# Two matmuls of 256 columns in place of one of 512, in the projections and the down products of a convolution and mixture-of-experts block

## The chip, the cores and the metric

The kernel runs on one core of one Trainium2 chip. The metric is the time of one execution on the device in microseconds (us); less is better. TensorE (PE in the profile) does the matmuls, and its weight loads have a row of their own (PEld). VectorE is DVE, ScalarE is ACT, GpSimd is POOL, and SyncE (SP) issues most of the DMAs.

## The reference, cut to what matters

There is one layer with 2048 tokens and 1024 channels, in float32: a gated short convolution between two projections, then a mixture of 16 experts, each of which takes the 256 tokens that score best for it.

```python
gate_b, gate_c, v = jnp.split(h @ w_in, 3, axis=-1)              # input projection, 1024 -> 3072
y = (gate_b * dwconv_centred(gate_c * v, conv_w)) @ w_out        # output projection, 1024 -> 1024
lat = lat + g1 * y
h2 = modulate(rms_norm(lat, norm_g[1]), sh2, sc2)
aff = jax.nn.softmax(h2 @ w_router)                              # 16 experts
g, idx = lax.top_k(jnp.swapaxes(aff, 1, 2), 256)
xs = h2[idx]                                                     # 256 rows for each expert
hid = jax.nn.silu(xs @ w_gate) * (xs @ w_up)                     # 1024 -> 1024, twice
ys = (hid @ w_down) * g                                          # 1024 -> 1024
lat = lat + g2 * scatter_add(ys, idx)
```

## The kernel before, in words

Every large product is made of three matmuls in the type fp32r: both operands are split into a rounded high part and the remainder, and high by high, high by low and low by high are added up in PSUM. `ws` tiles hold split weights, `hl` tiles the split activations of the mixer, `xT` and `hT` those of the experts. A matmul loads 128 columns of one operand into the array as weights (the stationary operand) and streams the columns of the other one past them (the moving operand). In the profile's `pm<-hl,ws` the first name is the moving operand and the second the stationary one.

- **Input projection** (`in_mm`, lines 436, 437, 439). For 32 combinations of a 128-channel block and a quarter of the tokens, eight steps k of nine products each: three weight matrices times three parts. Stationary: `ws`, 128x128. Moving: `hl`, 512 tokens. That is 2304 products. Each of the three outputs fills one PSUM bank of 512 float32 columns.
- **Output projection** (`out_mm`, lines 641, 642, 644). For 16 blocks of 128 tokens, eight steps of six products. Stationary: `hl`. Moving: `ws`, 512 columns. That is 768 products. Transposes (line 690) and the router's matmuls (lines 708 and 709, `hl` moving, 128 columns) stand between them.
- **Experts.** `gate_up` (lines 1010, 1012, 1014) has `ws` stationary and `xT`, 256 columns, moving: 6144 products. `down` (`product`, lines 1032 to 1034) has `hT` stationary and `ws`, 512 columns, moving: 1536 products in 32 calls. For each expert the order is half of `gate_up`, a `down` half of the expert before, the other half of `gate_up`, the other `down` half.

The order on every engine is that in which the code is written. The weights come by DMA into three buffers, are split by ACT (line 198) and DVE (line 208) into eight `ws` buffers, and are loaded some steps ahead of their use.

Of the kernel before, what the change touches and what calls it, by code (L numbers as in the profile page):

```python
# [21 lines left out]
KD = D // P  # L22
NB = L // P
NQ = 4
QT = L // NQ
# [15 lines left out]
def block_kernel(ctx: ExitStack, tc, x, c, ada_w, ada_b, norm_g, w_in, conv, w_out, router, wg, wu, wd, out):  # L41
    nc = tc.nc
# [57 lines left out]
    def constants(scratch):  # L100
        before = consts.tile([P, P], BF, name="before")
        nc.vector.tensor_scalar(before, jp, 0.0, None, op0=ALU.is_gt)
        ones_b = consts.tile([P, 1], BF, name="ones_b")
        nc.vector.memset(ones_b, 1.0)

        def group_of(name, shift, mask, pattern):

            row = consts.tile([P, 1], I32, name=name + "_i")
            nc.gpsimd.iota(row, pattern=[[0, 1]], base=0, channel_multiplier=1)
            nc.vector.tensor_scalar(row, row, shift, mask, op0=ALU.logical_shift_right, op1=ALU.bitwise_and)  # L110
            rowf = consts.tile([P, 1], F32, name=name + "_r")
            nc.vector.tensor_copy(rowf, row)
            n = 1
            for _, m in pattern:
                n *= m
            col = scratch("col", n)
            nc.gpsimd.iota(col, pattern=pattern, base=0, channel_multiplier=0, allow_small_or_imprecise_dtypes=True)
            t = consts.tile([P, n], F32R, name=name)
            nc.vector.tensor_scalar(t, col, rowf, None, op0=ALU.is_equal)
            return t, rowf  # L120

        same, _ = group_of("same", 3, E - 1, [[1, E], [0, 8]])
        sameq, _ = group_of("sameq", 3, NF - 1, [[0, P // (8 * NF)], [1, NF], [0, 8]])
        rep, repf = group_of("rep", 5, 3, [[1, 4]])
        block, _ = group_of("block", 5, 3, [[1, 4], [0, 32]])
        tri = consts.tile([P, P], BF, name="tri")
        nc.vector.tensor_mul(tri, block.bitcast(F32), before)
        mult = consts.tile([P, 5], F32, name="mult")
        nc.gpsimd.iota(mult, pattern=[[4, 5]], base=1, channel_multiplier=0, allow_small_or_imprecise_dtypes=True)
        nc.vector.tensor_scalar(mult, mult, repf, None, op0=ALU.add)  # L130
        stepq = consts.tile([P, N_FEW[0] + N_FEW[1], 3], F32, name="stepq")
        biasq = consts.tile([P, N_FEW[0] + N_FEW[1], 2], F32, name="biasq")
        for i in range(N_FEW[0] + N_FEW[1]):
            lo = i >= N_FEW[0]
            unit = 1.0 if lo else float(1 << LOW_FEW)
            st = unit * float(FEW) ** (N_FEW[0] + lo * N_FEW[1] - 1 - i)
            nc.gpsimd.tensor_scalar(stepq[:, i], mult[:, 0:3], st, None, op0=ALU.mult)
            nc.gpsimd.tensor_scalar(biasq[:, i], mult[:, 3:5], -st, 0.5 * unit, op0=ALU.mult, op1=ALU.add)
        needq = consts.tile([P, 5, 4], F32, name="needq")
        nc.gpsimd.memset(needq[:, 0:3], float(CAP))  # L140
        nc.gpsimd.memset(needq[:, 3:5], float(2 * CAP - L))
        slot_r = consts.tile([P, P], BF, name="slot_r")
        nc.gpsimd.iota(slot_r, pattern=[[1, P]], base=0, channel_multiplier=0,
                       allow_small_or_imprecise_dtypes=True)
        step = consts.tile([P, N_HI + N_LO], F32, name="step")
        bias = consts.tile([P, N_HI + N_LO, 2], F32, name="bias")
        for i in range(N_HI + N_LO):
            st = (1 << LOW) * 4.0 ** (N_HI - 1 - i) if i < N_HI else 4.0 ** (N_HI + N_LO - 1 - i)
            nc.gpsimd.memset(step[:, i:i + 1], st)
            for j in range(2):  # L150
                nc.gpsimd.memset(bias[:, i, j:j + 1], 0.5 * (float(1 << LOW) if i < N_HI else 1.0) - (j + 2) * st)
        need = consts.tile([P, 3], F32, name="need")
        nc.gpsimd.memset(need[:, 0:1], float(CAP))
        nc.gpsimd.memset(need[:, 1:3], float(2 * CAP - L))
        zero1 = consts.tile([P, 4], F32, name="zero1")
        nc.gpsimd.memset(zero1, 0.0)
        cnts = [consts.tile([P, 4], F32R, name=f"cnt{i}") for i in range(2)]
        for t in cnts:
            nc.vector.tensor_copy(t, zero1)
        zero1 = zero1[:, 0:1]  # L160
        aux = consts.tile([P, E, NB, 5], BF, name="aux")
        nc.gpsimd.iota(aux[:, :, :, 0], pattern=[[0, E], [0, NB]], base=0, channel_multiplier=1,
                       allow_small_or_imprecise_dtypes=True)
        nc.gpsimd.iota(aux[:, :, :, 1], pattern=[[0, E], [1, NB]], base=0, channel_multiplier=0,
                       allow_small_or_imprecise_dtypes=True)
        quick = sameq, rep, stepq, biasq, needq
        return before, ones_b, tri, slot_r, step, bias, need, zero1, cnts, aux, same, quick


    pieces, n_load, n_high, n_done = [], 0, 0, 0  # L170
# [177 lines left out]
    with tc.tile_pool(name="mix", bufs=1) as mix:  # L348
# [83 lines left out]
        def in_mm(ps, q, W, k):  # L432
            t = hl[q, k]
            for m in range(3):
                wh, wl = W(k, m)
                nc.tensor.matmul(ps[m], wh, t[:, 0], start=(k == 0), stop=False)  # L436
                nc.tensor.matmul(ps[m], wl, t[:, 0], start=False, stop=False)  # L437
            for m in range(3):
                nc.tensor.matmul(ps[m], W(k, m)[0], t[:, 1], start=False, stop=(k == KD - 1))  # L439

        def in_out(ps, q, ct):
            pb, pc, pv = ps
# [132 lines left out]
        for i, (ps_, ct, q) in enumerate(steps):  # L575
# [23 lines left out]
            ps = new_banks()  # L599
# [15 lines left out]
        def half(h):  # L615
            return slice(h * QT, (h + 1) * QT)
# [17 lines left out]
        def out_mm(tb, k, hs=(0, 1)):  # L634
            ps = ps_of.setdefault(tb, {})
            vh, vl = vs_of[tb]
            w = ws_of[w_o[k]]
            for h in hs:
                if k == 0:
                    ps[h] = mm.tile([P, QT], F32, name="pm", tag="mm")  # L640
                nc.tensor.matmul(ps[h], vh[:, k], w[:, 0, half(h)], start=(k == 0), stop=False)  # L641
                nc.tensor.matmul(ps[h], vh[:, k], w[:, 1, half(h)], start=False, stop=False)  # L642
            for h in hs:
                nc.tensor.matmul(ps[h], vl[:, k], w[:, 0, half(h)], start=False, stop=(k == KD - 1))  # L644

        def out_res(tb, h, soon=None):

# [378 lines left out]
    def down(e, dh, between=lambda kk: None):  # L1026
        ps = [mm.tile([P, H], F32, name="pm", tag="mm") for _ in range(2)]

        def product(s, k):
            w, j, t = ws_of[w_moe[2, e, dh, k // 2]], k % 2, slice(s * P, (s + 1) * P)  # L1030
            h, l = (hT_of[e][k // 4][:, i, k % 4, t] for i in range(2))
            nc.tensor.matmul(ps[s], h, w[:, 0, j], start=(k == 0), stop=False)  # L1032
            nc.tensor.matmul(ps[s], h, w[:, 1, j], start=False, stop=False)  # L1033
            nc.tensor.matmul(ps[s], l, w[:, 0, j], start=False, stop=(k == KD - 1))  # L1034

        for kk in range(KD // 2):
            between(kk)
            split_to(w_moe[2, e, dh, kk] + n_split - 1)
            if (e, dh) != (E - 1, 1):
                for k in (2 * kk, 2 * kk + 1):  # L1040
                    for s in range(2):
                        product(s, k)
        if (e, dh) == (E - 1, 1):
            for s in range(2):
                for k in range(KD):
                    product(s, k)
        if dh == 0:
            ot_of[e] = [moe.tile([P, D], F32, name="ot", tag="ot", bufs=3) for _ in range(2)]
        ots = ot_of[e]
        c0 = slice(dh * H, (dh + 1) * H)  # L1050
        for s in range(2):
            nc.vector.scalar_tensor_tensor(ots[s][:, c0], ps[s], gate_of[e][:, s:s + 1], g2b[:, c0],  # L1052
                                           op0=ALU.mult, op1=ALU.mult)
        if dh == 1:
            for s in range(2):
                if s:
                    nc.gpsimd.memset(spacer, 0.0)
                st = nc.gpsimd.indirect_dma_start(  # L1058
                    out=out_rows, out_offset=bass.IndirectOffsetOnAxis(ap=idx_of[e][:, s:s + 1], axis=0),
                    in_=ots[s], in_offset=None, compute_op=ALU.add)  # L1060
                if s == 0:
                    scat[e] = st
                else:
                    tc.declare_no_dep(st.ins, scat[e].ins, reason="an expert's rows are distinct")
# [61 lines left out]
```

## Time and profile before

| | |
|---|---|
| median of 3 runs | 1985.38 us (1983.81 to 1985.45) |
| profiled execution | 1985.33 us |
| its span, first to last instruction | 1983.5 us |
| TensorE busy, matmuls | 1901.4 us, 96% of the span |
| TensorE busy, weight loads | 1669.5 us, 84% |
| VectorE, ScalarE, GpSimd busy | 57%, 38%, 15% |
| mean granted TensorE clock | 0.982 |

The span is the profiler's; the 1.8 us between it and the execution's time lie around it. A matmul's busy time runs from its start to its modelled end, and a matmul starts while the one before it is still running, so the time that a product costs in a dense stretch is the distance from one start to the next. Some matmul records are missing from the trace, so such a distance is best taken from the first and the last row of a stretch with the number of products that the program has there.

### The profile page before, as it was taken

How to read it: one execution, taken by the hardware profiler on the slowest of the kernel's cores; microseconds unless marked ns; L12 is line 12 of the kernel's file. 1: busy time of each engine (PE TensorE's matmuls, PEld its weight loads, DVE VectorE, ACT ScalarE, POOL GpSimd, SP SyncE). 2: the span in 40 equal slices, each digit the busy share in tenths (PEclk: the TensorE clock that was granted, in tenths of full speed). 3: DMA queues.
4: the chain of work that ended last, by engine and by line, in shares of the span. 5: the costliest groups of instructions: out<-in, count | busy, mean ns of one | idle time of the engine just before them, and what ended most of it. 6: DMA issues, size and time to landing. Idle time of an engine off the chain costs nothing.

```text
span 1983.5 us, 29691 instructions
## 1 busy us (share of the span) xinstructions
PE 1901.4 (96%) x11930; PEld 1669.5 (84%) x11930; DVE 1130.6 (57%) x1656; ACT 751.2 (38%) x1050; POOL 306.9 (15%) x521
## 2 busy tenths in 40 slices
PE   4999999999999999659999999999999999999998
PEld 3787788887788888549999999999999999999996
DVE  7544424344334666776665656656665666566653
ACT  3411126211123333345444544444444444444542
POOL 3310011101011222333211011101110110111001
PEclk8999999999999999869999999999999999999999
DMA  9443241433216443235677676767677766777674
GB/s 283 127 133 127 81 144 53 139 127 123 67 64 213 166 149 132 85 127 165 199 222 211 214 233 200 220 217 235 202 214 233 227 201 214 229 209 218 212 212 116
DMA packets 216573, 344.38 MB, mean 174 GB/s; under 512 B 12092, under 2 KB 94068, under 8 KB 216436
## 3 DMA queue, kind: packets, MB, share of 16 engines
q1 hardware_dynamic: 200468, 284.82, 44.6%
q0 software_dynamic: 15968, 57.68, 11.2%
q8 instruction: 93, 1.52, 0.3%
q14 instruction: 44, 0.36, 0.1%
HBM read 300.51 MB, written 41.94 MB: 173 GB/s over the span
## 4 chain that ended last, share of the span: by engine, by line
PE 92%; DVE 3%; DMA 2%; SPq 1%; issue 1%; ACT 1%; POOL 0%; POOLq 0%; DVEq 0%; ACTq 0%
PE pm L1010 11%; PE pm L1012 11%; PE pm L1014 11%; PE pm L436 9%; PE pm L437 9%; PE pm L439 9%; PE pm L1032 6%; PE pm L1034 6%; PE pm L1033 6%; PE pm L641 3%; PE pm L644 3%; PE pm L642 3%; PE pt L986 1%; SPq L399 1%; DVE hl L312 1%
## 5 line engine op out<-in xcount | busy, mean ns | idle before, releaser
L208 DVE TENSOR_TENSOR ws<-raw,ws 128x1024 fp32r<-128x1024 f32 x415 | 499.0, 1223 | 314.4 <-ACT ws L198 312.5
L198 ACT ACTIVATE ws<-raw 128x1024 fp32r<-128x1024 f32 x437 | 451.0, 1054 | 444.2 <-PE pm L1014 208.0
L1010 PE MATMUL pm<-xT,ws 128*128 128x256 f32 x2048 | 569.6, 278 | 0.0
L1012 PE MATMUL pm<-xT,ws 128*128 128x256 f32 x2048 | 567.7, 277 | 0.1
L1014 PE MATMUL pm<-xT,ws 128*128 128x256 f32 x2048 | 567.4, 277 | 0.0
L1012 PEld LDWEIGHTS pm<-xT,ws 128*128 128x128 f32 x2048 | 386.4, 189 | 1.7 <-DVE xT L989 0.4
L1010 PEld LDWEIGHTS pm<-xT,ws 128*128 128x128 f32 x2048 | 386.2, 189 | 1.2
L1014 PEld LDWEIGHTS pm<-xT,ws 128*128 128x128 f32 x2048 | 386.0, 189 | 0.0
L436 PE MATMUL pm<-hl,ws 128*128 128x512 f32 x768 | 311.2, 405 | 1.0 <-ACT hl L386 1.0
L437 PE MATMUL pm<-hl,ws 128*128 128x512 f32 x768 | 307.0, 400 | 0.0
L439 PE MATMUL pm<-hl,ws 128*128 128x512 f32 x768 | 222.7, 398 | 0.0
L1032 PE MATMUL pm<-ws,hT 128*128 128x512 f32 x512 | 203.8, 398 | 0.0
L1034 PE MATMUL pm<-ws,hT 128*128 128x512 f32 x512 | 201.5, 394 | 0.0
L1033 PE MATMUL pm<-ws,hT 128*128 128x512 f32 x512 | 200.0, 391 | 0.0
L436 PEld LDWEIGHTS pm<-hl,ws 128*128 128x128 f32 x768 | 146.4, 191 | 36.6 <-ACT hl L386 1.4
L437 PEld LDWEIGHTS pm<-hl,ws 128*128 128x128 f32 x768 | 146.4, 191 | 35.1 <-issue 1.0
L439 PEld LDWEIGHTS pm<-hl,ws 128*128 128x128 f32 x768 | 145.8, 190 | 35.8
L1058 POOL DMA_INDIRECT out_dram<-ot,idx x32 | 78.5, 2454 | 591.4 <-DVE ot L1052 587.4
L449 DVE TENSOR_TENSOR u<-cs,pm 128x512 f32<-128x512 f32 x32 | 22.5, 703 | 246.0 <-ACT cs L446 246.0
L446 ACT ACTIVATE cs<-pm 128x512 f32<-128x512 f32 x32 | 19.1, 597 | 346.8 <-issue 272.0
L1034 PEld LDWEIGHTS pm<-ws,hT 128*128 128x128 f32 x512 | 96.2, 188 | 20.7
L1033 PEld LDWEIGHTS pm<-ws,hT 128*128 128x128 f32 x512 | 96.3, 188 | 18.9
(267 smaller groups left out, 2026.8 us busy)
## 6 DMA issues: line engine op xcount, KB each, us to landing
raw<-in_moe_w_gate_dram SPq DMA_DIRECT2D x128, 512.0 KB, 4.4
raw<-in_moe_w_up_dram SPq DMA_DIRECT2D x128, 512.0 KB, 4.3
raw<-in_moe_w_down_dram SPq DMA_DIRECT2D x128, 512.0 KB, 4.6
raw<-in_sc_w_in_dram SPq DMA_DIRECT2D x45, 512.0 KB, 4.6
xt<-in_x_dram SPq DMA_DIRECT2D x32, 512.0 KB, 6.2
aw<-in_ada_w_dram SPq DMA_DIRECT2D x32, 512.0 KB, 6.5
hl<-in_ada_w_dram SPq DMA_DIRECT2D x32, 256.0 KB, 5.4
hl<-vscr SPq DMA_DIRECT2D x16, 512.0 KB, 5.0
```

Source lines behind the costliest of these rows:

```text
L198: nc.scalar.activation(t[:, 0], raws[n_high], AF.Copy)
L208: (eng or nc.vector).tensor_sub(t[:, 1, ..., s], raw[..., s], t[:, 0, ..., s].bitcast(F32))
L436: nc.tensor.matmul(ps[m], wh, t[:, 0], start=(k == 0), stop=False)
L437: nc.tensor.matmul(ps[m], wl, t[:, 0], start=False, stop=False)
L439: nc.tensor.matmul(ps[m], W(k, m)[0], t[:, 1], start=False, stop=(k == KD - 1))
L1010: nc.tensor.matmul(o, w[:, 0, j, c0], xT[:, 0, k], start=(k == 0 and f % 2 == 0), stop=False, skip_group_check=True)
L1012: nc.tensor.matmul(o, w[:, 0, j, c0], xT[:, 1, k], start=False, stop=False, skip_group_check=True)
L1014: nc.tensor.matmul(o, w[:, 1, j, c0], xT[:, 0, k], start=False, stop=(k == KD - 1), skip_group_check=True)
L1032: nc.tensor.matmul(ps[s], h, w[:, 0, j], start=(k == 0), stop=False)
L1033: nc.tensor.matmul(ps[s], h, w[:, 1, j], start=False, stop=False)
L1034: nc.tensor.matmul(ps[s], l, w[:, 0, j], start=False, stop=(k == KD - 1))
L1058: st = nc.gpsimd.indirect_dma_start(out=out_rows, out_offset=bass.IndirectOffsetOnAxis(ap=idx_of[e][:, s:s + 1], axis=0), in_=ots[s], in_o ...
```

## The change

A helper issues a product as two matmuls: columns 0 to 255 of the moving operand into the first half of the PSUM tile, and columns 256 to 511 into the second, both with the same stationary operand. The flag that starts an accumulation is given to the first half alone. All 4608 products with 512 moving columns in the three places go through the helper. `gate_up`, the router, the transposes and all other engines are as before.

```diff
+    def mm_halves(o, w, v, start, stop):
+
+        for c in (slice(0, QT // 2), slice(QT // 2, QT)):
+            nc.tensor.matmul(o[:, c], w, v[:, c], start=start and c.start == 0, stop=stop, skip_group_check=True)
...
             for m in range(3):
                 wh, wl = W(k, m)
-                nc.tensor.matmul(ps[m], wh, t[:, 0], start=(k == 0), stop=False)
-                nc.tensor.matmul(ps[m], wl, t[:, 0], start=False, stop=False)
+                mm_halves(ps[m], wh, t[:, 0], k == 0, False)
+                mm_halves(ps[m], wl, t[:, 0], False, False)
             for m in range(3):
-                nc.tensor.matmul(ps[m], W(k, m)[0], t[:, 1], start=False, stop=(k == KD - 1))
+                mm_halves(ps[m], W(k, m)[0], t[:, 1], False, k == KD - 1)
...
-                nc.tensor.matmul(ps[h], vh[:, k], w[:, 0, half(h)], start=(k == 0), stop=False)
-                nc.tensor.matmul(ps[h], vh[:, k], w[:, 1, half(h)], start=False, stop=False)
+                mm_halves(ps[h], vh[:, k], w[:, 0, half(h)], k == 0, False)
+                mm_halves(ps[h], vh[:, k], w[:, 1, half(h)], False, False)
             for h in hs:
-                nc.tensor.matmul(ps[h], vl[:, k], w[:, 0, half(h)], start=False, stop=(k == KD - 1))
+                mm_halves(ps[h], vl[:, k], w[:, 0, half(h)], False, k == KD - 1)
...
-            nc.tensor.matmul(ps[s], h, w[:, 0, j], start=(k == 0), stop=False)
-            nc.tensor.matmul(ps[s], h, w[:, 1, j], start=False, stop=False)
-            nc.tensor.matmul(ps[s], l, w[:, 0, j], start=False, stop=(k == KD - 1))
+            mm_halves(ps[s], h, w[:, 0, j], k == 0, False)
+            mm_halves(ps[s], h, w[:, 1, j], False, False)
+            mm_halves(ps[s], l, w[:, 0, j], False, k == KD - 1)
```

## Rows read from the trace of the kernel before

**Rows 1.** The page: busy time by engine, and the chain that ended last.

```profile
PE 1901.4 (96%) x11930; PEld 1669.5 (84%) x11930; DVE 1130.6 (57%) x1656; ACT 751.2 (38%) x1050; POOL 306.9 (15%) x521
...
PE 92%; DVE 3%; DMA 2%; SPq 1%; issue 1%; ACT 1%; POOL 0%; POOLq 0%; DVEq 0%; ACTq 0%
```

**Rows 2.** Windows in the four dense stages: start:end, length, busy time (instructions), clock, DMA.

```profile
core 0: us, PE busy (x) PEld busy (x) DVE busy (x) ACT busy (x) POOL busy (x), PEclk, DMA share, GB/s
400.00:450.00 50.00, 50.00 (x213) 39.90 (x212) 20.40 (x23) 7.59 (x10) 4.12 (x11) 1.00 0.38 132
650.00:700.00 50.00, 50.00 (x279) 40.40 (x278) 30.74 (x58) 15.45 (x37) 12.96 (x42) 1.00 0.41 140
1300.00:1330.00 30.00, 30.00 (x237) 28.11 (x236) 16.82 (x20) 12.92 (x13) 1.97 (x2) 1.00 0.70 226
```

**Rows 3.** The chain in the input projection: start us, length us, what; 252 products between them.

```profile
376.75 0.71 PE pm L439 x3
...
435.79 0.71 PE pm L439 x3
```

**Rows 4.** Timeline of TensorE in the output projection: start, length; 12 products in a row.

```profile
818.59 0.40 PE L641 MATMUL pm<-ws,hl 128*128 128x512 f32 x1
818.83 0.39 PE L642 MATMUL pm<-ws,hl 128*128 128x512 f32 x1
...
821.16 0.39 PE L644 MATMUL pm<-ws,hl 128*128 128x512 f32 x1
```

**Rows 5.** Timeline of TensorE in a down half: 21 products in a row.

```profile
1200.21 0.39 PE L1032 MATMUL pm<-ws,hT 128*128 128x512 f32 x1
...
1204.79 0.40 PE L1034 MATMUL pm<-ws,hT 128*128 128x512 f32 x1
```

**Rows 6.** Timeline over a gate_up half: its first product, and the first after it.

```profile
1208.64 0.28 PE L1010 MATMUL pm<-xT,ws 128*128 128x256 f32 x1
1208.76 0.28 PE L1012 MATMUL pm<-xT,ws 128*128 128x256 f32 x1
...
1230.43 0.39 PE L1032 MATMUL pm<-ws,hT 128*128 128x512 f32 x1
```

**Rows 7.** Weight loads in a gate_up half, in the timeline of PEld.

```profile
1190.33 0.19 PEld L1010 LDWEIGHTS pm<-xT,ws 128*128 128x128 f32 x1
1190.45 0.19 PEld L1012 LDWEIGHTS pm<-xT,ws 128*128 128x128 f32 x1
1190.56 0.19 PEld L1014 LDWEIGHTS pm<-xT,ws 128*128 128x128 f32 x1
```

**Rows 8.** The page's groups for gate_up: instructions, busy us, mean ns of one.

```profile
L1010 PE MATMUL pm<-xT,ws 128*128 128x256 f32 x2048 | 569.6, 278 | 0.0
L1012 PE MATMUL pm<-xT,ws 128*128 128x256 f32 x2048 | 567.7, 277 | 0.1
...
L1012 PEld LDWEIGHTS pm<-xT,ws 128*128 128x128 f32 x2048 | 386.4, 189 | 1.7 <-DVE xT L989 0.4
L1010 PEld LDWEIGHTS pm<-xT,ws 128*128 128x128 f32 x2048 | 386.2, 189 | 1.2
```

**Rows 9.** Timeline over the end of gate_up(1, 1): 143 products between these two rows.

```profile
975.49 0.28 PE L1012 MATMUL pm<-xT,ws 128*128 128x256 f32 x1
...
992.34 0.40 PE L1032 MATMUL pm<-ws,hT 128*128 128x512 f32 x1
```

**Rows 10.** Timeline over the router's 16 matmuls of one token block: the first and the last.

```profile
815.66 0.22 PE L708 MATMUL plt<-hl,rts 128*32 128x128 f32 x1
...
816.56 0.22 PE L709 MATMUL plt<-hl,rts 128*32 128x128 f32 x1
```

**Rows 11.** The page: the DMA queue that carries TensorE's instructions; packets, MB, share.

```profile
q8 instruction: 93, 1.52, 0.3%
```

**Rows 12.** The window at the start, in the columns of rows 2.

```profile
16.00:48.00 32.00, 18.59 (x62) 14.10 (x63) 29.95 (x59) 11.87 (x17) 13.91 (x9) 0.78 1.13 290
```

## The prediction

> **What bounds the kernel now.** I read the busy table and the chain first: matmuls fill 96% of the span, and the chain that ended last is TensorE's for 92% of it [rows 1]. So what a product costs in TensorE's own stream goes straight into the time. The windows say the same by stage: in the input projection, the output projection and the experts TensorE is busy for the whole window at a granted clock of 1.00, which is 2.4 GHz, while DVE is busy for 41%, 61% and 56% of it and the DMA engines for 38% to 70% [rows 2]. No other engine is near to ending last there. Only at the start is TensorE waiting, busy for 18.59 of 32 us at a mean clock of 0.78 [rows 12]; some 60 matmuls lie there, and I leave them out.
>
> What a product costs is therefore the distance from start to start. I take it from first and last rows:
>
> - input projection, `hl` moving, 512 columns: 59.04 us for 252 products [rows 3], **234.3 ns**;
> - output projection, `hl` stationary, 512 columns: 2.57 us for 11 steps [rows 4], **233.6 ns**;
> - down, no `hl`, 512 columns: 4.58 us for 20 steps [rows 5], **229.0 ns**;
> - gate_up, no `hl`, 256 columns: 21.79 us for 192 products [rows 6], **113.5 ns**.
>
> At 2.4 GHz one column in each cycle would be 213.3 ns for 512 and 106.7 ns for 256. So every product carries an excess: 21.0, 20.3 and 15.7 ns at 512 columns, 6.8 ns at 256. The whole question is how this excess divides when a product is cut in two, for two matmuls of 256 columns stream as many columns as one of 512.
>
> **The change part by part.** It adds 2304 + 768 + 1536 = 4608 matmuls and as many weight loads. Nothing is moved in order, no wait is added, no DMA, and no other engine's instruction changes.
>
> *The weight loads.* Both halves use the same weights, but the second half will load them again: lines 1010 and 1012 use one and the same stationary operand one after the other, and both have their 2048 loads [rows 8]. Those loads last 188 to 189 ns and start every 113.5 ns, about as the matmul before them starts [rows 7, 8], so they lie under the running matmul. In the projections a half will have just this cover, one matmul of 256 columns. I cost the loads at nothing beyond the spacing that gate_up shows.
>
> A rule of the Trainium skill speaks against this: "TensorE: Matmul & The Clock Gate", Part 3, under "The mechanism", says that a weight load overlaps running matmuls only where it targets another row group. Loads of all 128 rows would then stand in line, and by the page's figure of columns over 1.2 GHz each of the 4608 would add an estimated 107 ns, 492 us in all. The trace doesn't agree: full-height loads start every 113.5 ns beside matmuls [rows 7].
>
> *The instructions.* TensorE's instruction queue moved 1.52 MB [rows 11] for 2 x 11930 instructions [rows 1], 64 bytes each. The change adds 9216, some 0.59 MB. In gate_up two instructions in each 113.5 ns are fed without a gap [rows 6], and the halves will ask for no more. Cost: nothing.
>
> *The halves.* No row shows a matmul of 256 columns with an `hl` operand. The bounds from rows:
>
> - Below: the spacing of gate_up, 113.5 ns a half, 227.0 a product.
> - Above: the excess that the stage's 512-column product shows belongs to each matmul, whatever its width. A half is then 106.7 + 21.0 = 127.7 ns in the input projection, 127.0 in the output projection, 122.4 in down.
>
> For down I take the lower bound: gate_up runs in the same part of the program, with `ws` on one side and an expert tile on the other. That is -2.0 ns a product, x 1536 = **-3.1 us**.
>
> For the projections I don't take it. Products of the same shape cost more wherever an `hl` tile is an operand: 5.3 ns more than in down as the moving one, 4.6 ns more as the stationary one. No engine's load explains it: DVE and the DMAs are less busy in the input projection than with the experts [rows 2]. It looks like something that a stream from or a load of such a tile costs. If it falls on every matmul, a half is 113.5 + 5.3 = 118.8 ns in the input projection, +3.3 ns a product, x 2304 = **+7.6 us**; and 113.5 + 4.6 = 118.1 ns in the output projection, +2.6, x 768 = **+2.0 us**. The one other row with `hl` moving fits. The router's 128 columns take 0.90 us for 15 steps, 60.0 ns [rows 10], 6.7 over the 53.3 that the columns need. A line through 128 columns at 60.0 and 512 at 234.3 passes 256 at 118.1. The value is nearer to these rows than to either bound.
>
> Sum: -3.1 + 7.6 + 2.0 = +6.5 us on the profiled 1985.33 (span 1983.5 and 1.8 around it; the median of the runs, 1985.38, is the same): **1992 us**, a little slower.
>
> **The rivals.**
>
> 1. *A half costs 113.5 ns everywhere.* For it: this is how nearly all of 6144 products of that shape run, each with its own load. Against it: none of them has an `hl` operand. Input projection -7.3 x 2304 = -16.8 us, output -6.6 x 768 = -5.1, down -3.1: -25.0, **1960 us**, faster. It decides once a half in the input projection is under 117.1 ns, half of 234.3.
> 2. *The slow rhythm.* The same matmuls of gate_up also run at another spacing: after a break at 975 us, 143 products took 16.85 us, 117.8 ns each, to the end of that half [rows 9]; the next halves are back at 113.5. If the halves fall into it, a product is 235.6 ns: +1.3 x 2304 + 2.0 x 768 + 6.6 x 1536 = +14.6 us, **2000 us**. It would be 26 us more if gate_up itself were held in it (4.3 ns x 6144).
> 3. *The excess goes with the columns.* Then cutting changes nothing in the projections: only down's -3.1 us is left, **1982 us**, the same.
> 4. *The excess belongs to each matmul*, the upper bound: 21.0 x 2304 + 20.3 x 768 + 15.7 x 1536 = +88 us, **2073 us**. Against it: gate_up's 6.8 ns, less than half of down's 15.7.
>
> By the section "Back-to-back issue gap" of the same page of the Trainium skill the spacing is columns over 2.4 GHz and about 2.5 ns for each matmul. The 4608 more matmuls would cost an estimated 11.5 us by that, which would end between my forecast and rival 2. The trace shows no such constant: 6.8 ns at 256 columns and 15.7 to 21.0 at 512.
>
> **How the numbers follow.** My forecast has a chance of 0.31, rival 1 of 0.27, rival 2 of 0.16, rival 3 of 0.14, rival 4 of 0.08, and 0.04 are left for something else, a slowdown. About 0.2%, 4 us, is what a measurement of this kernel can tell from no change. Of the forecast, which may miss by 5 us, I count 0.02 as faster, 0.07 as the same and 0.22 as slower; of rival 3, 0.06, 0.07 and 0.01; rival 1 is faster, all else slower. Faster: 0.27 + 0.02 + 0.06 = 0.35. Same: 0.14. Slower: 0.22 + 0.01 + 0.16 + 0.08 + 0.04 = 0.51. The range runs from just under rival 1 to beyond rival 2 with part of its spread into gate_up, 1957 to 2022; it leaves out rival 4, the rest and the edges, under 0.2. Cases of both signs hold much of the chance, so the likeliest one's own range: 1986 to 1997.
>
> **What would show it.** In the profile after, the groups of the helper's line should count 4608 matmuls and loads for `pm<-hl,ws`, 1536 for `pm<-ws,hl` and 3072 for `pm<-ws,hT`, all 128x256. In the input projection two rows of the chain that are 504 matmuls apart should stand 59.9 us apart; 57.2 is rival 1, 59.4 rival 2, 59.0 rival 3, 64.4 rival 4. A down half of 48 products should take 10.9 us against 11.0 before. Gate_up should stay at 113.5 ns. I am wrong if the halves settle at one spacing in all three places, or if a wait opens on TensorE that isn't there now: a half's weight load that starts late, or a gap in its instruction stream.

## The result and the profile after

The changed kernel takes **2003.19 us** (median of 4 runs, 2000.62 to 2004.66) against 1984.91 us on the same chip: a ratio of 1.0091 [1.0074, 1.0109], 18.3 us slower. The profiled execution took 2003.74 us, its span is 2001.9 us, and the mean granted clock 0.979 against 0.982.

The page after, its busy times, the instruction queue, the shares of the chain, and the groups of the helper's line (instructions, busy us, mean ns of one, idle before):

```profile
PE 1921.7 (96%) x16538; PEld 1905.5 (95%) x16538; DVE 1132.6 (57%) x1656; ACT 754.0 (38%) x1050; POOL 308.0 (15%) x521
...
q8 instruction: 129, 2.11, 0.4%
...
PE 92%; DVE 3%; DMA 1%; SPq 1%; issue 1%; ACT 1%; POOL 1%; POOLq 0%; DVEq 0%; ACTq 0%
...
L172 PE MATMUL pm<-hl,ws 128*128 128x256 f32 x4608 | 559.9, 283 | 1.0 <-ACT hl L391 1.0
L172 PEld LDWEIGHTS pm<-hl,ws 128*128 128x128 f32 x4608 | 553.4, 190 | 3.4 <-issue 1.9
L172 PE MATMUL pm<-ws,hT 128*128 128x256 f32 x3072 | 372.9, 280 | 0.0
L172 PE MATMUL pm<-ws,hl 128*128 128x256 f32 x1536 | 200.6, 286 | 0.0
```

TensorE is busy for 96% of the span and the chain is TensorE's for 92% of it, as in [rows 1]. There are 4608 more matmuls, and nothing new waits: the helper's groups have an idle time of 1.0 us in all. TensorE streams the same columns in 18 us more, with the granted clock all but the same. The windows of [rows 2] after the change show this by stage:

```profile
400.00:450.00 50.00, 50.00 (x424) 50.00 (x423) 20.70 (x23) 7.78 (x10) 4.12 (x11) 1.00 0.37 125
650.00:700.00 50.00, 50.00 (x443) 49.29 (x442) 33.64 (x59) 15.96 (x37) 11.77 (x35) 1.00 0.44 156
1300.00:1330.00 30.00, 30.00 (x277) 29.96 (x276) 16.43 (x20) 12.67 (x14) 1.97 (x2) 1.00 0.76 243
```

TensorE has no gap, its clock is at 1.00 (2.4 GHz), and in the first window it starts 424 matmuls where twice 213 would be the same work. So the time is in the spacing. The timeline after, of one long run in the input projection, one in the output projection, and two down halves (start, length, count):

```profile
350.29 102.78 PE L172 MATMUL pm<-hl,ws 128*128 128x256 f32 x864
...
663.54 3.11 PE L172 MATMUL pm<-ws,hl 128*128 128x256 f32 x24
...
1176.37 5.61 PE L172 MATMUL pm<-ws,hT 128*128 128x256 f32 x48
...
1182.22 5.90 PE L172 MATMUL pm<-ws,hT 128*128 128x256 f32 x48
1187.96 0.29 PE L1015 MATMUL pm<-xT,ws 128*128 128x256 f32 x1
...
1209.74 2.89 PE L172 MATMUL pm<-ws,hT 128*128 128x256 f32 x24
1212.46 1.03 PE L991 MATMUL pt<-identf,xs 128*128 128x128 f32 x8
1213.25 5.90 PE L172 MATMUL pm<-ws,hT 128*128 128x256 f32 x48
1219.00 1.03 PE L991 MATMUL pt<-identf,xs 128*128 128x128 f32 x8
1219.79 3.07 PE L172 MATMUL pm<-ws,hT 128*128 128x256 f32 x24
1222.70 0.29 PE L1015 MATMUL pm<-xT,ws 128*128 128x256 f32 x1
```

Such a row merges matmuls of one line. Its length runs to the end of the last one, 0.28 us after that one's start, and a run behind other matmuls begins with one distance of about 0.2 us. So the input projection's run gives (102.78 - 0.28 - 0.20) / 862 = 118.7 ns a half, and the output projection's (3.11 - 0.28 - 0.20) / 22 = 119.5 (119.8 over the whole stage). Down has two spacings. Straight out of gate_up, two runs differ by 24 halves and 5.61 - 2.89 us: 113.3 ns. Behind other matmuls (a few of the first down halves apart), 5.90 - 3.07 us for 24 halves: 117.9 ns. Gate_up's 192 matmuls from 1187.96 to 1209.74 take 113.4 ns each, as in [rows 6].

The chain after, between 100 and 160 us, is one piece of 507 matmuls, (60.17 - 0.28) / 506 = 118.4 ns each:

```profile
99.89 60.17 PE pm L172 x507
```

Summing the distances from start to start in the two traces by operands gives the whole difference. The two columns on the right are means over dense stretches, without the breaks:

| | before, us | after, us | | spacing before, ns | of a half after, ns |
|---|---|---|---|---|---|
| input projection | 557.7 | 563.2 | +5.5 | 234.2 | 118.7 |
| output projection | 187.4 | 193.5 | +6.1 | 233.4 | 119.8 |
| gate_up | 710.6 | 711.7 | +1.1 | 113.7 | 113.9 (not cut) |
| down | 356.0 | 361.4 | +5.3 | 229.3 | 116.4 |
| all else | 160.0 | 160.4 | +0.4 | | |

The sum, 18.4 us, is what lies between the two profiled executions (2003.74 and 1985.33). Gate_up's +1.1 us is no more than traces differ in that stage with nothing changed in it or in down: 710.6 us here, 708.8 and 707.8 in experiments 1 and 2.

### The profile page after: what moved, and what is told of

The parts are those of the page before. It is cut to its first block, busy times and chain, and to the rows that moved or that the text cites. A ratio compares the mean times of both kernels' runs of the same rounds, so it can differ in the third digit from the quotient of the medians.

```text
span 2001.9 us, 38903 instructions
## 1 busy us (share of the span) xinstructions
PE 1921.7 (96%) x16538; PEld 1905.5 (95%) x16538; DVE 1132.6 (57%) x1656; ACT 754.0 (38%) x1050; POOL 308.0 (15%) x521
## 3 DMA queue, kind: packets, MB, share of 16 engines
q8 instruction: 129, 2.11, 0.4%
## 4 chain that ended last, share of the span: by engine, by line
PE 92%; DVE 3%; DMA 1%; SPq 1%; issue 1%; ACT 1%; POOL 1%; POOLq 0%; DVEq 0%; ACTq 0%
PE pm L172 53%; PE pm L1015 11%; PE pm L1017 11%; PE pm L1019 11%; PE pt L991 1%; SPq L404 1%; DVE hl L317 1%; PE pt L695 1%; PE pt L388 1%; DMA xt<-in_x_dram 0%; PE plt L714 0%; PE plt L713 0%; PE pt L496 0%; PE pi L967 0%; DMA xs<-hscr,idx 0%
## 5 line engine op out<-in xcount | busy, mean ns | idle before, releaser
L172 PE MATMUL pm<-hl,ws 128*128 128x256 f32 x4608 | 559.9, 283 | 1.0 <-ACT hl L391 1.0
L172 PEld LDWEIGHTS pm<-hl,ws 128*128 128x128 f32 x4608 | 553.4, 190 | 3.4 <-issue 1.9
L172 PE MATMUL pm<-ws,hT 128*128 128x256 f32 x3072 | 372.9, 280 | 0.0
L172 PEld LDWEIGHTS pm<-ws,hT 128*128 128x128 f32 x3072 | 362.4, 188 | 0.0
L172 PE MATMUL pm<-ws,hl 128*128 128x256 f32 x1536 | 200.6, 286 | 0.0
L172 PEld LDWEIGHTS pm<-ws,hl 128*128 128x128 f32 x1536 | 189.2, 190 | 0.4
L975 POOL DMA_INDIRECT xs<-hscr,idx x32 | 33.3, 1041 | 339.9 <-issue 258.2
L1029 DVE TENSOR_TENSOR hT<-sg,hT 128x512 fp32r<-128x512 f32 x64 | 47.3, 740 | 44.7 <-ACT hT L1028 44.7
L213 POOL TENSOR_TENSOR ws<-raw,ws 128x1024 fp32r<-128x1024 f32 x22 | 53.4, 2433 | 69.7 <-ACT ws L203 60.2
L1028 ACT ACTIVATE hT<-sg 128x512 fp32r<-128x512 f32 x64 | 40.5, 632 | 58.8 <-DVE sg L1026 58.0
```

What stands on the lines that cost most here:

```text
L172: nc.tensor.matmul(o[:, c], w, v[:, c], start=start and c.start == 0, stop=stop, skip_group_check=True)
L213: (eng or nc.vector).tensor_sub(t[:, 1, ..., s], raw[..., s], t[:, 0, ..., s].bitcast(F32))
L975: nc.gpsimd.indirect_dma_start(out=xs, out_offset=None, in_=hscr, in_offset=bass.IndirectOffsetOnAxis(ap=idx[:, s:s + 1], axis=0))
L1028: nc.scalar.activation(hT[:, 0, t], sg, AF.Copy)
L1029: nc.vector.tensor_sub(hT[:, 1, t], sg, hT[:, 0, t].bitcast(F32))
```

## The experiments

Ratios are against the kernel before on the same chip. Spacings are from start to start in dense stretches. The first theory was that each stage pays for its own halves; then the question was what the excess of a matmul hangs on: the kind of its operands, as the prediction had it, where a tile begins, how far apart its two tiles begin, or the load beside the stream.

**1 to 3. One stage at a time.** The helper in one place, the products of 512 columns in the two others. For the first, one line of each group, against the changed kernel:

```diff
-                mm_halves(ps[h], vh[:, k], w[:, 0, half(h)], k == 0, False)
+                nc.tensor.matmul(ps[h], vh[:, k], w[:, 0, half(h)], start=(k == 0), stop=False)
...
-            mm_halves(ps[s], h, w[:, 0, j], k == 0, False)
+            nc.tensor.matmul(ps[s], h, w[:, 0, j], start=(k == 0), stop=False)
...
```

> Halves in the input projection alone. Theory A (each half pays its own stall, stage by stage, and nothing is carried on): the input projection alone gets longer, by the 5.5 us that its rows show after the change, and all later stages are as before; some 1990.5 us, ratio 1.003. Rival (the loss comes from the length of the instruction stream or is carried into later stages): more than 5.5 us, some of it behind the input projection.

> Halves in the output projection alone. Theory A: plus 6 us there and nothing elsewhere, some 1991 us, ratio 1.003; a product there goes from 233.6 to 239.8 ns. Rival (the half's price in the output projection depends on the rhythm that the input projection's halves leave behind): less than 3 us, a half near 117.

> Halves in down alone. Theory A: plus 6.4 us as in the whole change, of which 5.3 in down and 1.1 in gate_up, ratio 1.003: a half settles at 117.8 ns behind each break. Rival (113.5 ns is what a half costs here, as was predicted, and the slow spacing in the whole change was handed on from the stages before): minus 3 us, ratio 0.9985.

Measured: 1989.78, 1989.63 and 1990.44 us against 1983.43; ratios 1.0032 [1.0020, 1.0045], 1.0031 [1.0019, 1.0044], 1.0035 [1.0021, 1.0048]. That is +6.35, +6.2 and +7.0 us, 19.6 together against 18.3 for the whole change. Each stage pays its own part. A stage on which nothing was changed keeps its spacing, and down loses without the projections' halves.

The trace of the first shows that the input projection's halves have two spacings as well:

```profile
84.89 84.72 PE L172 MATMUL pm<-hl,ws 128*128 128x256 f32 x720
...
170.77 68.91 PE L172 MATMUL pm<-hl,ws 128*128 128x256 f32 x576
```

The first stretch begins with a distance of 0.20 us, the second, behind longer matmuls, with one of 0.52: (84.72 - 0.28 - 0.20) / 718 = 117.3 ns and (68.91 - 0.28 - 0.52) / 574 = 118.7 ns a half.

**4 and 5. 32 bytes ahead of `hl`.** An unused tile moves all `hl` tiles by 32 bytes; nothing else changes. Once in the kernel before, once in the changed one.

```diff
+        pad = mix.tile([P, 8], F32, name="pad")
+        nc.gpsimd.memset(pad, 0.0)
```

> The kernel before, products of 512 columns, with one more tile of 32 bytes ahead of the hl tiles, so that they begin on a multiple of 64 bytes and not 32 bytes past one. Theory B (the excess of the stages with hl comes from where the tile begins): input projection from 234.3 to about 229 ns, output projection from 233.6 to about 229, as in down, whose tiles all begin on a multiple of 64: minus 12 and minus 3.5 us, some 1969 us, ratio 0.992. Rival (it is the stage, its other engines or the kind of product): no change, ratio 1.000.

> The changed kernel (halves everywhere) with the hl tiles 32 bytes further on, on multiples of 64. Theory B (a tile that begins 32 bytes past a multiple of 64 costs every matmul a stall): halves in both projections fall to the spacings of gate_up, 117.8 ns at the most (minus 4 us in the input and minus 3 in the output projection against the changed kernel, some 1996) and 113.4 at the best (minus 24 and minus 10, some 1969). Rival (the address matters to streams of 512 columns alone): 118.7 and 119.9 ns stay, some 2003.

Measured for the kernel before: 1977.52 us, 0.9971 [0.9959, 0.9984]. The output projection falls from 233.4 to 229.45 ns, 228.8 in steady stretches, which is down's spacing; the input projection only from 234.2 to 233.3, where theory B had about 229. Two rows of its timeline show the former, 12 products apart (2.74 us, 228.3 ns):

```profile
817.20 0.39 PE L646 MATMUL pm<-ws,hl 128*128 128x512 f32 x1
...
819.94 0.39 PE L646 MATMUL pm<-ws,hl 128*128 128x512 f32 x1
```

Measured for the changed kernel: 1982.92 us, 20 us less than without the pad and 0.9992 [0.9983, 1.0001] of the kernel before. The output projection's halves go to 117.8, the input projection's to gate_up's pair of spacings. Its timeline there:

```profile
279.76 21.70 PE L172 MATMUL pm<-hl,ws 128*128 128x256 f32 x190
...
339.81 102.01 PE L172 MATMUL pm<-hl,ws 128*128 128x256 f32 x864
441.65 1.88 PE L498 MATMUL pt<-acc,ones_f 128*128 128x512 f32 x4
442.97 68.40 PE L172 MATMUL pm<-hl,ws 128*128 128x256 f32 x576
511.21 1.88 PE L498 MATMUL pt<-acc,ones_f 128*128 128x512 f32 x4
512.52 82.19 PE L172 MATMUL pm<-hl,ws 128*128 128x256 f32 x720
```

The first run is (21.70 - 0.28) / 189 = 113.3 ns a half, the second (102.01 - 0.28 - 0.20) / 862 = 117.8. The last two follow the same four matmuls of line 498, and one runs at (68.40 - 0.28 - 0.52) / 574 = 117.8, the other at (82.19 - 0.28 - 0.52) / 718 = 113.4. So an `hl` operand costs nothing by itself; where the tile lies does.

**6. 32 bytes ahead of the experts' tiles** `xT` and `hT`, in the kernel before.

```diff
+    pad2 = moe.tile([P, 8], F32, name="pad2")
+    nc.gpsimd.memset(pad2, 0.0)
```

> The kernel before with the expert tiles xT and hT moved 32 bytes on, off the multiples of 64 on which they begin. Theory B: gate_up, whose moving tile is xT, goes from 113.5 to 118.7 ns (as the halves with a moving hl), 6144 times, plus 32 us; down, whose stationary tile is hT, from 229.0 to 233.6, plus 7 us; some 2022 us, ratio 1.019. Rival (only the stages with hl have it): no change, ratio 1.000.

Measured: 2016.1 us, 1.0160 [1.0145, 1.0176]. Gate_up, which no edit to the matmuls touches, goes from 113.7 to 118.3 ns, +25 us; down from 229.3 to 233.2, +5.9. Its timeline over one gate_up half, 192 products in 22.73 us:

```profile
1176.88 0.28 PE L1012 MATMUL pm<-xT,ws 128*128 128x256 f32 x1
...
1199.61 0.39 PE L1034 MATMUL pm<-ws,hT 128*128 128x512 f32 x1
```

**7. All starts of `hl`.** The 16 `hl` buffers are made 32 bytes longer, so that they begin at every multiple of 32 within 512 bytes. One execution; the lines that shape the buffers' views are left out here.

```diff
-            return mix.tile(shape, dt, name="hl", tag="hl", bufs=16)
+            t = mix.tile([P, D + 8], F32, name="hl", tag="hl", bufs=16)
...
```

> The kernel before with hl buffers that are 32 bytes longer, so that the 16 buffers begin at every multiple of 32 within 512 bytes; the step k of the input projection uses one buffer after the other. Theory B (only the multiple of 64 counts): steps alternate between two spacings, 234.3 and 233.3 ns. Rival C (the distance between the moving and the stationary tile within 512 bytes counts, as it would where two streams meet in the same bank): the spacing differs from step to step in a pattern of 8 or 16, with steps at 229 or under.

Measured: 1981.4 us. The input projection's mean spacing by the start of the `hl` tile that it streams, for the start in 512 and for the one 256 bytes further:

| start of `hl`, mod 256 | 0 | 32 | 64 | 96 | 128 | 160 | 192 | 224 |
|---|---|---|---|---|---|---|---|---|
| ns | 231.9, 232.2 | 234.2, 233.5 | 233.0, 232.8 | 233.4, 232.7 | 228.3, 227.3 | 233.3, 233.4 | 230.6, 230.9 | 233.2, 234.2 |

Starts 256 bytes apart agree within 1 ns, and the least is at 128, where `ws` begins too. (A buffer serves 9 products in a row, so passages from one to the next are in these means.)

**8. Less load beside the stream.** In the input projection and in down, the two products with a low part load 32 of the 128 stationary columns (the second of them not in the last step of a sum), so 96 of 128 output rows miss these low parts. One execution; one of the edited lines:

```diff
-                nc.tensor.matmul(ps[m], wl, t[:, 0], start=False, stop=False)
+                nc.tensor.matmul(ps[m][0:32], wl[:, 0:32], t[:, 0], start=False, stop=False)
...
```

> The kernel before, where in the input projection and in down the products with a low part load 32 of their 128 stationary columns (but for the last step of a sum): the low parts then reach only 32 of 128 rows of the output, the rest of it lacks them. The load of a product runs beside the stream of the product before it. Theory D (the excess over 213.3 ns comes from the weight load beside the stream): products beside a load of 32 columns lose most of their excess, to 217 to 220 ns, and those beside a full load stay at 229 and 234. Rival (the stream has the excess by itself): 229 and 234 everywhere.

Measured: 1987.27 us. The loads did get shorter, from 190 to 110 ns in the input projection:

```profile
L436 PEld LDWEIGHTS pm<-hl,ws 128*128 128x128 f32 x768 | 146.0, 190 | 92.0 <-issue 3.0 <-ACT hl L386 1.6
...
L437 PEld LDWEIGHTS pm<-hl,ws 128*32 128x32 f32 x768 | 84.2, 110 | 34.8 <-issue 1.0
```

But the input projection is at 231.5 ns against 234.2, and down at 232.8 against 229.3, one a little better and one worse. Single distances beside a short load lie between 225 and 238, like those beside a full one; none comes near 217 to 220. The length of the loads is not where the excess comes from.

**9 and 10. Everything at 128.** `hl` 96 bytes and the experts' tiles 64 bytes further, so that `ws`, `hl`, `xT` and `hT` all begin at 128 modulo 256; in the kernel before, and in the changed one.

```diff
+        pad = mix.tile([P, 24], F32, name="pad")
+        nc.gpsimd.memset(pad, 0.0)
...
+    pad2 = moe.tile([P, 16], F32, name="pad2")
+    nc.gpsimd.memset(pad2, 0.0)
```

> The kernel before (products of 512) with the hl tiles 96 bytes and the expert tiles 64 bytes further on, so that ws, hl, xT and hT all begin 128 bytes past a multiple of 256. Theory C (the distance of moving and stationary tile within 256 bytes sets the excess, and zero is the best, as in the scan's buffers at 128 and 384): input projection 227 ns (minus 17 us), output projection 227 (minus 5), down 227 (minus 3), gate_up 113.4 as now or a little less; some 1959 us, ratio 0.987. Rival B (only multiples of 64 count): as with the shift by 32, input 233.3, output and down 229, some 1978, ratio 0.997.

> The changed kernel with the same two shifts. Theory C: no stall is left for a half to pay, halves at 113.4 ns everywhere, the same time as the kernel of 512 columns with these shifts within 4 us, some 1959, ratio 0.987. Rival (a cut costs something for each matmul whatever the addresses, or the halves fall into the spacing of 117.8): 10 to 40 us above that, 1970 to 2000.

Measured for the kernel before: 1999.04 us, 1.0074 [1.0061, 1.0088]. Products of 512 columns reach 226.7 ns in all three places, the input projection alone saving 17.3 us, but gate_up goes to 120.0 and loses 35. The timeline, over 29 steps of nine products of the input projection and over a gate_up half:

```profile
360.28 0.39 PE L438 MATMUL pm<-hl,ws 128*128 128x512 f32 x1
...
419.44 0.39 PE L438 MATMUL pm<-hl,ws 128*128 128x512 f32 x1
...
1195.94 0.28 PE L1014 MATMUL pm<-xT,ws 128*128 128x256 f32 x1
...
1218.97 0.40 PE L1036 MATMUL pm<-ws,hT 128*128 128x512 f32 x1
```

59.16 us / 261 = 226.7 ns; 23.03 us / 192 = 119.9 ns. Measured for the changed kernel: 2052.01 us, 1.0347 [1.0333, 1.0361], and every matmul of 256 columns at 120.0 ns. Its timeline in the input projection, (103.92 - 0.28 - 0.20) / 862 = 120.0:

```profile
354.00 103.92 PE L172 MATMUL pm<-hl,ws 128*128 128x256 f32 x864
```

So here the excess is 13.3 ns a matmul at either width: 213.3 + 13.3 and 106.7 + 13.3. That is the law of the prediction's rival 4, and cutting a product in two costs 13.3 ns. For 4608 products that is 61 us; the two kernels are 53 us apart, since the short stretches of the output projection and of down, uncut, start above 226.7 (228.6 and 228.0 ns in the mean). My expectation that a half would have no excess left at this distance fell.

**11. All tiles 32 bytes further**, the distances between them kept; the kernel before. This tells the place of a tile from the distance between two.

```diff
+    pad0 = consts.tile([P, 8], F32, name="pad0")
+    nc.gpsimd.memset(pad0, 0.0)
```

> The kernel before with 32 bytes ahead of all tiles, so that ws, hl, xT and hT move together: every distance between a moving and a stationary tile stays, and all four leave or reach a multiple of 64. Theory C (the distance counts): 234.3, 233.4, 229.0 and 113.4 ns as before, 1984 us, ratio 1.000. Rival B (the multiple of 64 counts): gate_up and down, now both off it, go to 118.5 and 234 ns, plus 31 and plus 8 us, some 2020 us, ratio 1.019.

Measured: 1983.99 against 1984.21 us, 1.0000 [0.9990, 1.0009], and the same spacing in each stage (234.2, 233.4, 113.6, 229.3). Its timeline over a down stretch, 10 products and 2.29 us:

```profile
1204.66 0.39 PE L1035 MATMUL pm<-ws,hT 128*128 128x512 f32 x1
...
1206.95 0.39 PE L1036 MATMUL pm<-ws,hT 128*128 128x512 f32 x1
1207.18 0.28 PE L1012 MATMUL pm<-xT,ws 128*128 128x256 f32 x1
```

That is 229 ns, where experiment 6, with `hT` 32 bytes further alone, has 233.2. It is the distance.

**12. The better distance where there are 512 columns.** `hl` and `hT` at 128 like `ws`, `xT` left where it was; the kernel before. The first two lines are those of experiment 9.

```diff
+        pad = mix.tile([P, 24], F32, name="pad")
+        nc.gpsimd.memset(pad, 0.0)
...
+        if (e, fh) == (0, 0):
+            pad2 = moe.tile([P, 16], F32, name="pad2")
+            nc.gpsimd.memset(pad2, 0.0)
```

> The kernel before (512 columns) with hl 96 bytes and hT 64 bytes further on, at distance 0 from ws, and xT left where it was, 64 bytes short of it. Theory C with what the last two runs showed (distance 0 gives 226.7 ns at 512 columns but 120.0 at 256; 64 bytes short gives 113.4 at 256): input projection minus 17 us, output minus 3 to 5, down minus 2, gate_up unchanged: some 1961 us, ratio 0.988. Rival (the shift of gate_up's neighbours or another address moves gate_up to 117.8 or 120 as well): 1985 us or more.

Measured: 1985.93 us, 1.0009 [1.0000, 1.0018]. In its trace the 14.8 us won in the input projection, 2.6 in down and 1.3 in the output projection are lost again in gate_up, +23.3, though its own tiles lie as before. The traced execution is the slowest of 11 (1990.96 us; the others 1983.46 to 1988.01), so gate_up may lose some us less in the others. Its timeline over one half, 192 products in 22.62 us, 117.8 ns:

```profile
1198.14 0.28 PE L1012 MATMUL pm<-xT,ws 128*128 128x256 f32 x1
...
1220.64 0.28 PE L1016 MATMUL pm<-xT,ws 128*128 128x256 f32 x1
1220.76 0.39 PE L1037 MATMUL pm<-ws,hT 128*128 128x512 f32 x1
```

These halves follow a down half in the rhythm of 226.7 ns and keep the slower of gate_up's two spacings to their end, the one of [rows 9]. The fastest kernel measured is that of experiment 4. `hl` alone at 128 was not run; by the stages measured here it would save an estimated 15 to 17 us in the input projection (experiments 12 and 9). That gate_up would stay as it is, as with the shift of `hl` by 32 bytes, is not shown.

## Why the prediction was right, and where it was not

The direction and the range held: 1992 us forecast with 1957 to 2022, 2003.2 measured. It was 11 us short, outside the likeliest case's own range of 1986 to 1997. The "slower" in it hung on the two terms for the projections alone, and the reason given for them was wrong, so that it came out is in part luck. By its steps:

- **TensorE's stream bounds the kernel: right.** The change of the dense spacings alone, times the products, is 7.4 + 4.8 + 5.4 = 17.5 us of the 18.4.
- **Loads and instructions at nothing: right in that nothing queues.** The instruction queue moved 2.11 - 1.52 = 0.59 MB more, as worked out. The full-height loads do lie under running matmuls. Whether a half pays part of its excess for its own load stays open (below). The rule cited there, "TensorE: Matmul & The Clock Gate", Part 3 of the Trainium skill, would have made the kernel an estimated 492 us slower; the measured 18.3 us leaves no room for that. The same section of the Trainium skill also lets a load run ahead into a background weight buffer, which the prediction left out. So it did with the other section it cites: there the Trainium skill keeps columns over 2.4 GHz plus 2.5 ns for a matmul by itself and says that a stream of loads and matmuls departs from it. Here it does, upward: 226.7 to 234.2 ns at 512 columns, against an estimated 215.8 by that formula.
- **Input projection, +7.6 us: right in size.** 118.8 ns forecast, 118.7 measured. By the chain 504 of them take 59.7 us, where 59.9 was forecast. The stage pays 5.5 us in the whole trace and 6.35 alone. The reason was wrong, so that the size fits is luck: it is not that a tile is an `hl` tile. With 32 bytes ahead of them the same tiles stream at gate_up's 113.3 or 117.9 ns (experiment 5).
- **Output projection, +2.0 us: too small by 4.** A half took 119.8 ns, not 118.1. Adding the 4.6 ns of a 512-column product to gate_up's 113.5 had no ground: experiment 4 removes this 4.6 by 32 bytes, and the halves then are at 117.8, not at 113.5.
- **Down, -3.1 us: the step that failed.** "For down I take the lower bound" gave down's halves gate_up's spacing, since both have `ws` on one side and an expert tile on the other. Only the halves that run straight out of gate_up have it, 113.3 ns; behind the transposes and the small matmuls inside the down halves they run at 117.9. Down loses 5.3 us in place of winning 3.1. The 117.9 is rival 2's slow rhythm, and the mis-sizing of this term, 8.4 us, is most of the 11 that were missing.
- **Gate_up stays at 113.5: right.** Its +1.1 us is within what traces differ by. Behind a slow down half it falls back to 113.3 ns after some two matmuls, as in 21.78 us for 192 from 1187.96; two of its halves in this trace stay at 117.8, as one long stretch did before [rows 9].
- **Rivals.** Rival 1 needs all halves at 113.5; the input projection shows such stretches only with another distance (experiment 5). Rival 2 (2000 us) came nearest in time, though the projections are not at its 117.8. Rivals 3 and 4 lie on either side: a half's excess is 12.0, 13.1 and (behind other matmuls) 11.2 ns where the whole product's was 21.0, 20.3 and 15.7 [rows 3 to 5], so cutting leaves 57 to 71% of it on each half, not 50% and not 100%.

What stays open: why the distance between two tiles sets the spacing, whether the time is lost in the moving reads or beside them, and what decides which of two spacings a stream of the same form settles in. Experiment 8 speaks against the length of the loads alone. One more thing is in the trace of the kernel before: behind a wait of TensorE, where the granted clock is 0.50 (1.2 GHz), the excess is gone at both widths. Two windows, and the timeline in each:

```profile
34.00:37.00 3.00, 3.00 (x9) 2.32 (x8) 2.96 (x10) 1.77 (x3) 0.20 (x1) 0.50 1.17 290
877.50:880.00 2.50, 2.50 (x13) 2.50 (x13) 0.96 (x7) 1.09 (x4) 0.00 (x0) 0.50 0.03 7
...
34.24 0.63 PE L437 MATMUL pm<-hl,ws 128*128 128x512 f32 x1
...
36.37 1.39 PE L439 MATMUL pm<-hl,ws 128*128 128x512 f32 x3
...
877.51 0.41 PE L1012 MATMUL pm<-xT,ws 128*128 128x256 f32 x1
...
880.07 0.41 PE L1012 MATMUL pm<-xT,ws 128*128 128x256 f32 x1
```

Five products of 512 columns take 2.13 us, 426 ns each, and 12 of 256 take 2.56 us, 213.3 ns each; columns over 1.2 GHz are 426.7 and 213.3. So the excess is not a time that each matmul pays whatever the clock.

## What to carry to other kernels

Two matmuls of half the width cost more here than one, since each pays its own excess (11 to 13 ns after the change), except where the stream ran in the rhythm of 113.3 ns. Before cutting or joining matmuls in a stage that TensorE fills, take the start-to-start distance from the trace and compare it with columns over the clock; then look at where the two operands start in SBUF, because 32 bytes moved this kernel by -6 to +32 us. Do not carry the spacing of one stage to another on the likeness of shapes alone.

## What the runs showed of the hardware that was not expected

The spacing of these fp32r matmuls, with a load of 128 columns for each, depends, at a granted clock of 1.00, on the distance between the starts of the moving and of the stationary operand modulo 256 bytes (experiments 6, 7 and 11). In the built program before, `ws` begins at 128, `hl` at 32, `xT` and `hT` at 64, and all slices begin at multiples of 256 bytes within their tiles. Steady spacings or stage means, ns:

| moving less stationary, mod 256 | 512 columns | 256 columns |
|---|---|---|
| 0 | 226.7 (exp. 9, three stages) | 120.0 (exp. 9 and 10) |
| 32 | 233.2 (down, exp. 6) | |
| 64 | 229.0 (down before), 228.8 (output, exp. 4) | 117.8 (output, exp. 5); 113.3 or 117.9 (down after) |
| 96 | 233.4 (output before) | 119.8 (output after) |
| 160 | 234.2 (input before) | 118.7 (input after), 117.3 in stretches (exp. 1) |
| 192 | 233.3 (input, exp. 4) | 113.3 or 117.8 (gate_up; input, exp. 5) |
| 224 | | 118.3 (gate_up, exp. 6) |

Empty cells were not run as a stage. For 512 columns experiment 7 gives all eight distances in one stage, its start less 128: in order from 0, 228.3, 233.3, 230.6, 233.2, 231.9, 234.2, 233.0 and 233.4 ns, passages included. The order is not the same for the two widths: of the distances run, the one that is best for 512 columns is the worst for 256. And two spacings occur for one shape at one distance, 113.3 and 117.8 ns, or 117.3 and 118.7 at 160. One of them can hold for 864 matmuls (experiment 5). What the stream came out of has a part in it (down after the change, gate_up in experiment 12), but is not all: behind the same matmuls experiment 5 has one stretch at 117.8 and one at 113.4.
